# An attention's value products in one 65-column block of one bank, and a group's end in three instructions

## The chip, the core and the metric

The kernel runs on one core of one Trainium2 chip. The metric is device time in microseconds (us) of one execution. Five queues matter: TensorE (PE, with PEld for its weight loads), VectorE (DVE), ScalarE (ACT), GpSimd (POOL) and SyncE (SP), which issues most of the DMAs.

## The reference, cut to what matters

The program is one layer of an encoder on 2048 tokens of width 1024: an RMSNorm, one combined projection, latent attention with 12 heads (queries and keys of 64 + 32 rotary dimensions, values of 64), a small cross-attention to 256 memory rows, a silu gate, an output projection, the residual and a last RMSNorm. All in float32. What the change touches is this:

```
s = (einsum('bqhd,bkhd->bhqk', qn, k_nope) + einsum('bqhr,bkr->bhqk', qr, k_rope)) * scale
p = softmax(s, axis=-1)
attn = einsum('bhqk,bkhd->bqhd', p, v)
branch = concatenate([attn, mem_out], axis=-1) * silu(gate)
```

## The kernel before, in words

To keep float32's accuracy with float16 operands, every operand is split into a high part (the value rounded to float16) and a low part (what is left), and a product is made of three: high by high, high by low, low by high.

The work has three stages. First come the projections, the gate (its silu is written into float32 tiles A, 128 x 4 x 256 for each chunk of 512 tokens) and the memory heads. Then comes the latent attention, here read as the stretch from 461 to 1600 us. Last comes the output projection, to the end.

The attention runs over 48 groups: 6 pairs of heads, 4 chunks of 512 queries, 2 heads. A group has 16 units, one for each 128 keys. A unit (`scores`, then `pv` three units later) does this:

- Three 512-column matmuls make the scores of 128 keys by 512 queries in one bank (tag sc, three banks).
- ACT takes the exponential twice, once to float16 (the high part) and once to float32. Then DVE, or GpSimd in three units of eight, subtracts one from the other: the low part. In the trace this is a 128x512 TENSOR_TENSOR B<-B.
- The value product follows for each of the unit's four blocks of 128 queries. The high part is the stationary operand against 129 columns (64 of v's low part, 64 of v's high part, one column of a constant for the softmax's sum), and the low part against the last 65 of these. A tile of 129 columns per block results, two blocks to a bank, so a group holds both banks of the tag pv.

Beside the units, the groups ahead are prepared: 16 matmuls with 16 TENSOR_REDUCEs on DVE find the row maxima of the next group (tag m, three banks), and the next pair's keys, values and queries are projected (`prep_k`, `prep_v`, `prep_q_steps`), with ACT and DVE writing the high and low parts. GpSimd also splits the output projection's weights.

A group ends in `evac` once its last unit is added up. For each of the two banks ACT copies the low-part columns into a tile sm, DVE takes the reciprocal of the sums, DVE adds the high-part columns to sm, and then two SCALAR_TENSOR_TENSORs on DVE multiply each block by its reciprocal and by the gate tile, in place. The pair's banks come free when the two additions have read them.

The order on each engine is made at build time by a scheduler that lists the instructions against its own estimate of time; each engine then runs its list strictly in order. Matmuls go out in that order too (line 116 records them all, line 91 every instruction of DVE, ACT and GpSimd).

Of the kernel before, what the change touches and what calls it, by code (L numbers as in the profile page):

```python
# [9 lines left out]
F32 = mybir.dt.float32  # L10
# [3 lines left out]
ALU = mybir.AluOpType  # L14
# [3 lines left out]
P = 128  # L18
# [10 lines left out]
VD = 64  # L29
# [12 lines left out]
TPC = CH // P  # L42
# [3 lines left out]
XS = 16.0  # L46
XW = 1.0 / (XS * WS)
BS = 1.0 / 16.0
X_PART = {0: ((0, slice(0, 256)),), 1: ((0, slice(256, 1024)),), 2: ((1, slice(0, 512)),), 3: ((1, slice(512, 1024)),)}
X_JOIN = 2  # L50
DVE_TO = 4
# [19 lines left out]
def kernel(ctx: ExitStack, tc: tile.TileContext, a, out: bass.AP):  # L71
# [26 lines left out]
    vec, act, gps = Ordered(nc.vector), Ordered(nc.scalar), Ordered(nc.gpsimd)  # L98
# [6 lines left out]
    def T(tag, shape, dt):  # L105
        cnt[0] += 1
        return sb.tile(shape, dt, tag=tag, bufs=TAGS[tag], name=f"{tag}_{cnt[0]}")

    def PT(tag):
        cnt[0] += 1  # L110
        return ps.tile([P, 512], F32, tag=tag, bufs=TAGS[tag], name=f"ps_{tag}_{cnt[0]}")
# [3 lines left out]
    def mm(o, lhsT, rhs, start, stop):  # L115
        ins = nc.tensor.matmul(o, lhsT, rhs, start=start, stop=stop, skip_group_check=True)  # L116
        if strict[0]:
            tc.keep_in_program_order(ins)
        return ins
# [6 lines left out]
    def stt(o, i0, s, i1, op0, op1):  # L126
        vec.scalar_tensor_tensor(out=o, in0=i0, scalar=s, in1=i1, op0=op0, op1=op1)
# [79 lines left out]
        gps.tensor_tensor(pa, t2, c, op=ALU.mult)  # L207
        gps.tensor_tensor(t2, pa, pc, op=ALU.add)

# [1 line left out]
    gcol = sb.tile([P, 2 * NK], F32, name="gcol")  # L211
    nc.sync.dma_start(gcol, a["gcols"])
    junk = sb.tile([P, QL], BF16, name="junk")
# [53 lines left out]
        act.activation(ctab.rearrange("p t f -> p (t f)"), kf, AF.Sin)  # L267


# [1 line left out]
    ops = {}  # L271

    def hilo(dst, src, eng):
# [62 lines left out]
            ins = mm(o, hi[:, js_], wh, False, stop and j == 3)  # L336
        return ins

# [1 line left out]
    W1 = [T("B", [P, 2, NW1], F16) for _ in range(NK)]  # L340
    hTs = {}
    A = {}
# [127 lines left out]
            for o, i in late.pop(0)[1]:  # L470
                tc.keep_in_program_order(nc.sync.dma_start(o, i, transpose=True))

# [1 line left out]
    kmem = [None]  # L474
    vmem = [None]
    wms = {}
# [25 lines left out]
    def mem_acc(h, q):  # L502
        if h == 0 and q == 0:
            kmem[0] = T("V", [NOPE + 1, 2, 2, 2, NMEM], F16)
            gps.memset(kmem[0][NOPE:NOPE + 1, :, :, 0, :], -MROW)
            vmem[0] = T("cn", [P, 2, MHEADS, 2 * VD + 1], F16)
            gps.memset(vmem[0][:, :, :, 2 * VD:2 * VD + 1], 1.0 / BS)
        if q == 0:
# [90 lines left out]

    def pv(g, u):  # L600
        if u == 0:
            g.pv = [PT(g.pvtag), PT(g.pvtag)]
        phl = g.p.pop(u)
        last = u == g.nkeys // P - 1
        vl, vh = g.v(u)
        W = 2 * VD + 1
        for qt in range(TPC):
            o = g.pv[qt // 2]
            b = (qt % 2) * W
            mm(o[:, b:b + W], phl[:, 0, qt * P:(qt + 1) * P], vl, u == 0 and qt % 2 == 0, False)  # L610
            mm(o[:, b + VD:b + W], phl[:, 1, qt * P:(qt + 1) * P], vh, False, last)

    def norm_pair(o3):
        sm = T("sm", [P, 2, VD], F32)
        rc = T("st", [P, 2, 1], F32)
        acopy(sm, o3[:, :, 0:VD])
        vec.reciprocal(rc, o3[:, :, 2 * VD:2 * VD + 1])
        vec.tensor_tensor(sm, o3[:, :, VD:2 * VD], sm, op=ALU.add)
        return [(j, sm[:, j, :], rc[:, j, :]) for j in range(2)]

    def evac(g):
        W = 2 * VD + 1
        at = a_tile(g.c, g.col // 256)
        for i in range(2):
            o3 = g.pv[i][:, 0:2 * W].rearrange("p (q w) -> p q w", q=2)
            for j, sm, r in norm_pair(o3):
                gs = at[:, i * 2 + j, g.col % 256:g.col % 256 + VD]
                stt(gs, sm, r, gs, ALU.mult, ALU.mult)

    LAG = 3  # L630

# [26 lines left out]
    def mem_steps(t):  # L658
        st = {}
        W = 2 * VD + 1  # L660

# [76 lines left out]
    Vt = {}  # L738
# [37 lines left out]
    def alloc_v(p):  # L776
        Vt[p] = [T("V", [P, NT, 2 * VD + 1], F16) for _ in range(2)]
        for hd in range(2):
            gps.memset(Vt[p][hd][:, :, 2 * VD:2 * VD + 1], 1.0 / BS)

# [84 lines left out]
    def mla_group(p, hd, c):  # L865
        g = Group()
        g.kd = QKD
        g.c, g.col = c, (p * 2 + hd) * VD
        g.nkeys, g.dim, g.scale = SEQ, QKD, SC_MLA
        hi, lo = Kt[p][hd]  # L870
        g.khi = lambda o, n, e=0: hi[0:QKD + e, o:o + n]
        g.klo = lambda o, n: lo[0:QKD, o:o + n]
        qt = Qt[(p, hd, c)]
        g.qhi, g.qlo = qt[:, 0, :], qt[:, 1, :]
        g.v = lambda u: (Vt[p][hd][:, u, :], Vt[p][hd][:, u, VD:2 * VD + 1])
        g.p = {}
        g.last = (p, hd, c) == (NPAIR - 1, 1, NCH - 1)
        g.pvtag, g.sctag = "pv", "sc"
        g.alloc = mla_alloc
        return g  # L880
# [1 line left out]
    krT[:] = [T("B", [P, SEQ], F16), T("B", [P, SEQ], F16)]  # L882
    fq, hq = [], []

# [9 lines left out]
            if f is not None:  # L894
                f()

# [1 line left out]
    Wg = {}  # L898
    wgt, wgr, wgs = {}, {}, {}
    scr = {"b": dram.tile([P, 4, 3, 2, 512], F16, name="scr_b")}  # L900
# [126 lines left out]
    def reload_A(j, c):  # L1027
        nc.sync.dma_start(a_tile(c, j), spill[c, j - 1])

# [1 line left out]
    first = {}  # L1031

    def first_max():
# [166 lines left out]
            lambda: put("S4", comb(a12, a12, a11, ALU.subtract), gps),  # L1200
        ]

# [1 line left out]
    order = [(p, hd, c) for p in range(NPAIR) for c in range(NCH) for hd in range(2)]  # L1204
    cur = first["g"]
    wo_in = a["w_out_l0"]
# [67 lines left out]
    for n in range(12):  # L1274
        c, j = n % NCH, 1 + n // NCH
        wo_at.setdefault(A_AT[j] + c, []).append((0, lambda j=j, c=c: reload_A(j, c)))
    for n, name in enumerate(WO_BLK):
        g = (41 if n < 4 else 46) + n % 2
# [8 lines left out]
    for gi, (p, hd, c) in enumerate(order):  # L1287
        slots = [[] for _ in range(16)]
        j = gi % 8
# [4 lines left out]
        if hd == 0 or gi == len(order) - 7:  # L1294
            if hd:
                np_, nc_ = p, 2
            if np_ < NPAIR and nc_ < NCH:
                st = prep_q_steps(np_, nc_)
# [35 lines left out]
            cur = hold["g"]  # L1334
    stream.flush()

# [1 line left out]
    SC = IWS / BS  # L1338

    chain = [None]  # L1340
# [18 lines left out]
    for i in range(NT // 2):  # L1359
        strict[0] = i > 0  # L1360
        t0, t1 = 2 * i, 2 * i + 1
        last = i == NT // 2 - 1
# [36 lines left out]
    i, t0, t1 = NT // 2 - 1, NT - 2, NT - 1  # L1399
# [75 lines left out]
```

## Time and profile before

| | |
|---|---|
| median of 3 runs | 1766.88 us (1765.35 to 1768.74) |
| span of the profiled execution, first to last instruction | 1761.3 us |
| difference between the two | 5.6 us |
| busy over the span: PE, DVE, ACT, POOL | 95%, 84%, 73%, 53% |
| attention, 461 to 1600 us | 1139 us |
| granted clock of TensorE over the span / in the attention | 0.988 / 1.00 |

The span is of one profiled execution; the runs were timed apart from it, so the 5.6 us hold what lies before the first and after the last instruction and the spread of the runs. A matmul's row lasts until its last result is written, while the next one already streams, so PE's busy share is higher than the share of time in which it streams.

### The profile page before, as it was taken

Reading aid. Unit: us, or ns where it says so; the run is one execution under the profiler, and the core shown is the slowest. Engines: PE = TensorE matmul, PEld = TensorE weight load, DVE = VectorE, ACT = ScalarE, POOL = GpSimd, SP = SyncE. Lnnn points to the kernel's source line nnn. Section 1 sums busy time; section 2 is a strip of 40 time slices with the busy share of each in tenths; the row PEclk is TensorE's granted clock in tenths of the full one; section 3 lists DMA queues with packets and bytes.
Section 4 is the critical chain, followed back from the end, with each engine's and each line's share of the span. In section 5 each row is a group of like instructions: output and inputs, shape, how many; then the busy total and the mean of one; then the engine's idle time right before and its main releaser. Section 6 shows DMA issues by size and latency. Waiting matters only on the chain.

```text
span 1761.3 us, 38122 instructions
## 1 busy us (share of the span) xinstructions
PE 1677.2 (95%) x14292; PEld 935.8 (53%) x14292; DVE 1471.3 (84%) x2785; ACT 1279.6 (73%) x2642; POOL 926.3 (53%) x1211
## 2 busy tenths in 40 slices
PE   7999999989999999999999999999999999998997
PEld 3554544435455565566555655556556555554443
DVE  6777658777889889998999898988999889987775
ACT  6776657776788778878787777877888778884332
POOL 2766444443355556566665665555344455435553
PEclk9999989999999999999999999999999999999999
DMA  8753350221301012111211132113001134105774
GB/s 291 212 167 111 77 148 25 84 103 49 85 14 25 22 50 72 35 38 23 61 22 38 22 86 34 37 23 95 13 13 37 38 96 97 25 25 124 189 194 141
DMA packets 187034, 133.95 MB, mean 76 GB/s; under 512 B 140193, under 2 KB 162849, under 8 KB 186849
## 3 DMA queue, kind: packets, MB, share of 16 engines
q1 hardware_dynamic: 186560, 130.74, 28.2%
q8 instruction: 111, 1.82, 0.4%
q10 hardware_dynamic: 288, 0.79, 0.1%
q14 instruction: 75, 0.61, 0.1%
HBM read 69.89 MB, written 25.17 MB: 54 GB/s over the span
## 4 chain that ended last, share of the span: by engine, by line
PE 52%; DVE 23%; DMA 8%; ACT 8%; issue 5%; POOL 3%; SPq 0%; DVEq 0%; ACTq 0%; POOLq 0%
PE ps_sc L116 27%; PE ps_pv L116 13%; PE ps_m L116 12%; DVE B L91 11%; DVE st L91 9%; ACT B L91 6%; DMA W<-V 3%; DMA V<-in_x_dram 1%; POOL B L91 1%; DVE V L91 1%; DMA B<-V 1%; DMA W<-B 1%; DVE W L91 1%; DVE sm L91 1%; POOL V L91 1%
## 5 line engine op out<-in xcount | busy, mean ns | idle before, releaser
L116 PEld LDWEIGHTS <-B 128*128 128x128 f16 (+2 forms) x9720 | 638.0, 98 | 504.5 <-issue 47.2
L91 ACT ACTIVATE B<-ps_sc 128x512 f16<-128x512 f32 x1529 | 794.7, 619 | 142.8 <-PE ps_pv L116 84.8
L91 POOL TENSOR_TENSOR B<-B 128x512 f16<-128x512 f32 (+1 forms) x328 | 392.6, 1201 | 495.3 <-ACT B L91 420.1
L116 PE MATMUL ps_sc<-W,B 96*128 96x512 f16 (+1 forms) x2304 | 627.4, 379 | 6.3 <-ACT B L91 3.7
L91 DVE TENSOR_REDUCE st<-ps_m 128x1 f32<-128x512 f32 (+1 forms) x800 | 525.8, 680 | 72.6 <-PE ps_m L116 69.8
L91 DVE TENSOR_TENSOR B<-B 128x512 f16<-128x512 f32 (+1 forms) x494 | 400.7, 819 | 42.1 <-ACT B L91 34.7
L116 PE MATMUL ps_pv<-V,B 128*128 128x129 f16 (+1 forms) x6144 | 384.6, 207 | 16.9 <-DVE B L91 9.7
L116 PEld LDWEIGHTS <-W 128*128 128x128 f16 (+2 forms) x2164 | 205.3, 99 | 236.9 <-issue 38.4
L116 PE MATMUL ps_m<-B,W 96*128 96x512 f16 x768 | 273.6, 381 | 13.7 <-DVE st L91 11.2
L116 PE MATMUL ps_sc<-B,B 128*128 128x512 f16 (+1 forms) x912 | 212.6, 371 | 11.2 <-ACT B L356 6.5
L116 PE MATMUL ps_sc<-B,W 128*128 128x512 f16 x648 | 156.6, 391 | 13.5 <-DVE cn L91 8.3
L91 POOL TENSOR_TENSOR B<-B,B 128x256 f16<-128x256 f32 (+3 forms) x112 | 110.3, 985 | 88.0 <-DVE B L91 80.2
L91 ACT ACTIVATE W<-ps_m 1x512 f16<-1x512 f32 (+2 forms) x144 | 78.1, 542 | 59.9 <-PE ps_m L116 25.0
L91 ACT ACTIVATE B<-B 128x512 f32<-128x512 f32 (+4 forms) x132 | 79.8, 643 | 31.5 <-DVE B L91 15.3
L91 ACT ACTIVATE V<-B 128x256 f16<-128x256 f32 x112 | 40.8, 413 | 75.5 <-DMA W<-V 36.2
L116 PE MATMUL ps_m<-cT,W 128*128 128x512 f16 x360 | 87.7, 383 | 0.0
L116 PE MATMUL ps_sc<-cT,W 128*128 128x512 f16 (+1 forms) x312 | 71.7, 381 | 6.4 <-DVE B L91 6.4
L91 DVE SCALAR_TENSOR_TENSOR B<-sm,st,B 128x64 f32<-128x64 f32 x192 | 73.9, 432 | 0.0
L91 POOL TENSOR_TENSOR st<-st,mhalf 128x1 f32<-128x1 f32 x66 | 42.4, 643 | 58.5 <-DVE st L91 55.9
L116 PE MATMUL ps_m<-W,cT 128*128 128x64 f16 (+1 forms) x1440 | 71.4, 203 | 0.0
L116 PEld LDWEIGHTS <-cT 128*128 128x128 f16 x1440 | 64.5, 98 | 10.9
L91 POOL TENSOR_TENSOR V<-B,V 128x256 f16<-128x256 f32 x70 | 52.5, 768 | 31.9 <-ACT V L91 31.7
(123 smaller groups left out, 1554.0 us busy)
## 6 DMA issues: line engine op xcount, KB each, us to landing
B<-in_xT_dram SPq DMA_DIRECT2D x16, 512.0 KB, 7.3
V<-in_x_dram SPq DMA_DIRECT2D x16, 512.0 KB, 5.3
B<-in_x_dram SPq DMA_DIRECT2D x16, 512.0 KB, 4.7
V<-in_xT_dram SPq DMA_DIRECT2D x14, 512.0 KB, 4.1
wo_scr<-B SPq DMA_DIRECT2D x56, 128.0 KB, 2.0
out_dram<-B SPq DMA_DIRECT2D x14, 512.0 KB, 3.2
spill<-B SPq DMA_DIRECT2D x12, 512.0 KB, 2.8
B<-spill SPq DMA_DIRECT2D x12, 512.0 KB, 3.8
```

The lines of the kernel that those rows point to most:

```text
L91: ins = f(*args, **kw)
L116: ins = nc.tensor.matmul(o, lhsT, rhs, start=start, stop=stop, skip_group_check=True)
```

## The change

`pv` makes three products for each block of queries instead of two, all into the same 65 columns: high by v's high part and the sum's column (65 columns), high by v's low part (64 columns), low by v's high part (65 columns). The four blocks of a group lie side by side in one bank (4 x 65 = 260 columns), so a group holds one bank of the tag pv and not two. `evac` becomes one reciprocal over the four sums and one TENSOR_TENSOR on DVE that multiplies the four blocks by the gate tile, and one TENSOR_TENSOR on GpSimd that multiplies the result by the reciprocals. ACT has no part in a group's end any more. `norm_pair` stays for the memory heads. The columns streamed for a block are 129 + 65 = 194 before and 65 + 64 + 65 = 194 now; the matmuls and weight loads of the attention's value products go from 6144 to 9216 each.

```diff
+PVW = VD + 1
...
     def pv(g, u):
         if u == 0:
-            g.pv = [PT(g.pvtag), PT(g.pvtag)]
+            g.pv = PT(g.pvtag)
         phl = g.p.pop(u)
         last = u == g.nkeys // P - 1
         vl, vh = g.v(u)
-        W = 2 * VD + 1
         for qt in range(TPC):
-            o = g.pv[qt // 2]
-            b = (qt % 2) * W
-            mm(o[:, b:b + W], phl[:, 0, qt * P:(qt + 1) * P], vl, u == 0 and qt % 2 == 0, False)
-            mm(o[:, b + VD:b + W], phl[:, 1, qt * P:(qt + 1) * P], vh, False, last)
+            b = qt * PVW
+            o = g.pv[:, b:b + PVW]
+            hi, lo = phl[:, 0, qt * P:(qt + 1) * P], phl[:, 1, qt * P:(qt + 1) * P]
+            mm(o, hi, vh, u == 0 and qt == 0, False)
+            mm(g.pv[:, b:b + VD], hi, vl, False, False)
+            mm(o, lo, vh, False, last)
...
     def evac(g):
-        W = 2 * VD + 1
         at = a_tile(g.c, g.col // 256)
-        for i in range(2):
-            o3 = g.pv[i][:, 0:2 * W].rearrange("p (q w) -> p q w", q=2)
-            for j, sm, r in norm_pair(o3):
-                gs = at[:, i * 2 + j, g.col % 256:g.col % 256 + VD]
-                stt(gs, sm, r, gs, ALU.mult, ALU.mult)
+        gs = at[:, :, g.col % 256:g.col % 256 + VD]
+        o3 = g.pv[:, 0:TPC * PVW].rearrange("p (q w) -> p q w", q=TPC)
+        rc = T("st", [P, TPC, 1], F32)
+        vec.reciprocal(rc, o3[:, :, VD:PVW])
+        vec.tensor_tensor(gs, o3[:, :, 0:VD], gs, op=ALU.mult)
+        gps.tensor_tensor(gs, gs, rc.to_broadcast([P, TPC, VD]), op=ALU.mult)
...
-        g.v = lambda u: (Vt[p][hd][:, u, :], Vt[p][hd][:, u, VD:2 * VD + 1])
+        g.v = lambda u: (Vt[p][hd][:, u, 0:VD], Vt[p][hd][:, u, VD:2 * VD + 1])
```

The scheduler lists the instructions anew. On DVE, this is the end of the 22nd of the 48 groups before (ps_pv_13237 and ps_pv_13238 are the group's two banks, sm the tiles of the additions, st_13556 the row maxima of the next group, B_9006 the gate tile):

```order
L91 RECIPROCAL st_13597<-ps_pv_13237 128x2
L91 TENSOR_TENSOR sm_13596<-ps_pv_13237,sm_13596 128x128
L91 RECIPROCAL st_13604<-ps_pv_13238 128x2
L91 TENSOR_TENSOR sm_13603<-ps_pv_13238,sm_13603 128x128
L91 TENSOR_REDUCE st_13556<-ps_m_13700 128x1
L91 TENSOR_REDUCE st_13556<-ps_m_13703 128x1
L91 SCALAR_TENSOR_TENSOR B_9006<-sm_13596,st_13597,B_9006 128x64 x2
L91 TENSOR_REDUCE st_13556<-ps_m_13721 128x1
L91 SCALAR_TENSOR_TENSOR B_9006<-sm_13603,st_13604,B_9006 128x64 x2
L91 TENSOR_REDUCE st_13556<-ps_m_13740 128x1
```

And the end of the same group now, on DVE (ps_pv_14350 is its bank, st_14724 the row maxima of the next group, B_5246 to B_5249 the exponentials whose low parts are taken, B_9538 the gate tile):

```order
L92 TENSOR_REDUCE st_14724<-ps_m_14750 128x1
L92 RECIPROCAL st_14772<-ps_pv_14350 128x4
L92 TENSOR_TENSOR B_9538<-ps_pv_14350,B_9538 128x4x64
L92 TENSOR_TENSOR B_5247<-B_5247 128x512
L92 TENSOR_REDUCE st_14724<-ps_m_14827 128x1
L92 TENSOR_TENSOR B_5248<-B_5248 128x512
```

Eight instructions of the group's end have become two, and the two stand behind the third TENSOR_REDUCE of the next group, where the eight began behind the fifth.

On GpSimd the multiply by the reciprocals stands between the pieces of the weights' split, the next queries' rotation and the low parts, here at the same group's end (B_9538 is the gate tile, cn_14813 the queries' rotation, B_14043 and B_14463 the output projection's weights, B_5246 and B_5249 low parts of exponentials):

```order
L92 TENSOR_TENSOR B_14463<-B_14043,B_14463 128x256
L92 TENSOR_TENSOR B_5246<-B_5246 128x512
L92 TENSOR_TENSOR B_14043<-B_14043 128x256
L92 TENSOR_TENSOR B_9538<-B_9538,st_14772 128x4x64
L92 TENSOR_TENSOR cn_14813<-cn_14813,ctab 128x128
L92 TENSOR_TENSOR cn_14813<-cn_14813,stab 128x128 x2
L92 TENSOR_TENSOR B_5249<-B_5249 128x512
```

The row of B_9538 is new in this queue: it waits for DVE's multiply, and the rotation and the low part of B_5249 stand behind it.

## Rows read from the trace of the kernel before

**Rows 1.** The page: the chain that ended last, shares of the span.
```profile
PE 52%; DVE 23%; DMA 8%; ACT 8%; issue 5%; POOL 3%; SPq 0%; DVEq 0%; ACTq 0%; POOLq 0%
```
**Rows 2.** Busy time in the attention (stretch, its length; each engine's busy us; clock).
```profile
461.00:1600.00 1139.00, 1099.72 (x10987) 654.49 (x10986) 1025.37 (x1859) 911.12 (x1878) 623.01 (x651) 1.00 0.18 43
```
**Rows 3.** PE's instructions by form, 461 to 1600 us (count, busy us, mean ns, idle).
```profile
L116 PE MATMUL ps_m<-B,W 96*128 96x512 f16 x745 | 264.5, 380 | 13.7 <-DVE st L91 11.2 <-ACT W L91 0.7 <-DVE V L91 0.2
L116 PE MATMUL ps_m<-cT,W 128*128 128x512 f16 x327 | 78.4, 379 | 0.0
L116 PE MATMUL ps_m<-W,cT 128*128 128x128 f16 x480 | 32.7, 219 | 0.0
L116 PE MATMUL ps_m<-W,cT 128*128 128x64 f16 x792 | 30.1, 193 | 0.0
L116 PE MATMUL ps_m<-ident,st 128*1 128x128 f16 x188 | 18.0, 218 | 4.3 <-DVE st L91 2.6 <-DVE B L91 1.6
```
**Rows 4.** The same without splitting by form: the scores and the value products.
```profile
L116 PE MATMUL ps_sc<-W,B 96*128 96x512 f16 x2295 | 624.4, 379 | 4.7 <-ACT B L91 3.7
L116 PE MATMUL ps_pv<-V,B 128*128 128x129 f16 (+1 forms) x6144 | 384.6, 207 | 16.9 <-DVE B L91 9.7 <-ACT B L91 3.6 <-POOL B L91 2.1
```
**Rows 5.** PE's timeline at four places (start us, us, what, count).
```profile
649.81 0.95 PE L116 MATMUL ps_m<-W,cT 128*128 128x64 f16 x27
...
901.83 1.67 PE L116 MATMUL ps_m<-cT,W 128*128 128x512 f16 x7
...
906.10 0.51 PE L116 MATMUL ps_pv<-V,B 128*128 128x129 f16 x8
906.45 0.38 PE L116 MATMUL ps_sc<-W,B 96*128 96x512 f16 x1
```
**Rows 6.** Sum over 47 stretches: 9 us from each group's first reciprocal.
```profile
sum 423.00, PE 396.83 PEld 234.83 DVE 422.37 ACT 325.30 POOL 274.79; mean PE 8.44 PEld 5.00 DVE 8.99 ACT 6.92 POOL 5.85
```
**Rows 7.** Sum over 47 stretches: the 3 us after those.
```profile
sum 141.00, PE 140.13 PEld 85.07 DVE 135.77 ACT 111.58 POOL 73.21; mean PE 2.98 PEld 1.81 DVE 2.89 ACT 2.37 POOL 1.56
```
**Rows 8.** Waits of PE and its loads, 461 to 1600 us (total us, times, longest).
```profile
PE ps_m L116 <- DVE st L91: 13.8, 42, 1.2
...
PEld L116 <- DVE B L91: 37.8, 70, 1.8
...
PEld L116 <- ACT B L91: 8.5, 19, 0.7
```
**Rows 9.** The timeline behind the 22nd group's end.
```profile
989.26 0.96 DVE L91 SCALAR_TENSOR_TENSOR B<-sm,st,B 128x64 f32<-128x64 f32 x2
...
990.75 0.61 DVE L91 SCALAR_TENSOR_TENSOR B<-sm,st,B 128x64 f32<-128x64 f32 x2
990.88 0.38 PE L116 MATMUL ps_m<-B,W 96*128 96x512 f16 x1 [0.46 <-DVE st L91]
```
**Rows 10.** DVE's, ACT's and GpSimd's instructions by form, 461 to 1600 us.
```profile
L91 DVE RECIPROCAL st<-ps_pv 128x2 f32<-128x2 f32 x96 | 15.3, 159 | 2.9 <-ACT sm L91 2.0
...
L91 DVE TENSOR_TENSOR sm<-ps_pv,sm 128x128 f32<-128x128 f32 x96 | 25.7, 268 | 0.0
...
L91 DVE SCALAR_TENSOR_TENSOR B<-sm,st,B 128x64 f32<-128x64 f32 x189 | 71.4, 425 | 0.0
...
L91 ACT ACTIVATE sm<-ps_pv 128x128 f32<-128x128 f32 x96 | 23.6, 325 | 6.0 <-PE ps_pv L116 6.0
...
L91 DVE SCALAR_TENSOR_TENSOR V<-ps_m,V 128x256 f16<-128x256 f32 x40 | 16.6, 414 | 0.0
...
L91 DVE SCALAR_TENSOR_TENSOR W<-ps_m,W 64x512 f16<-64x512 f32 x46 | 31.5, 685 | 11.2 <-ACT W L91 10.5
...
L91 POOL TENSOR_TENSOR B<-B 128x256 f32<-128x256 f32 x34 | 33.2, 976 | 0.0
```
**Rows 11.** Low parts on DVE: all, and one on the timeline.
```profile
L91 DVE TENSOR_TENSOR B<-B 128x512 f16<-128x512 f32 x480 | 395.1, 830 | 42.1 <-ACT B L91 34.7 <-issue 3.2 <-PE ps_sc L116 1.5
...
1040.09 0.68 DVE L91 TENSOR_TENSOR B<-B 128x512 f16<-128x512 f32 x1
```

## The prediction

> **What bounds the kernel now.** I read the chain of waits first. PE holds 52% of it and DVE 23% [rows 1], so the question is how often PE has to wait for DVE. The change touches the attention alone, 1139 us [rows 2]; the other stages keep their code. There PE shows 1099.7 us busy, which looks like 39 us of idleness. But a matmul's row is longer than its place in the stream. Seven 512-column matmuls take 1.67 us of rows, so one follows the other after (1.67 - 0.38) / 6 = 0.215 us, while its own row lasts 0.38 [rows 5]. So I count the stream itself [rows 3, 4]:
>
> - 2295 + 745 + 327 matmuls of 512 columns at 0.215 us: 723.9 us.
> - 768 units of value products. One unit's eight start at 906.10 and the next matmul at 906.45 [rows 5], 0.35 us: 268.8 us.
> - 792 of 64 columns. 27 of them take 0.95 us of rows, (0.95 - 0.19) / 26 = 0.029 us each [rows 3, 5]: 23.1 us.
> - 480 + 188 of 128 columns, an estimate of 0.056 us each (64 more columns at the 512-column rate, 0.215 / 512 us, on top of 0.029): 37.4 us.
>
> The sum is 1053 us, so PE stands still for some 86 of the 1139, 2.2 times what its busy time shows. Most of the waits that are named are for DVE: 37.8 and 13.8 us, against 8.5 for ACT [rows 8].
>
> Where does it stand still? I cut out 9 us from each group's end, 47 times. DVE is busy there for 422.4 of 423 us and PE shows 26.2 us of idleness. In the 3 us that follow it shows 0.9 of 141, or 2.6 in 423 [rows 6, 7]. So 24 of the 39 us shown stand behind a group's end, with DVE full. By the factor of 2.2 that is an estimate of 50 us really lost there. One such place: four SCALAR_TENSOR_TENSORs stand between the row maxima, and PE waits 0.46 us for a maximum at 990.88, while DVE multiplies blocks by gates [rows 9].
>
> **The change, part by part.** The parts are PE's products, the end of a group on DVE, on ACT and on GpSimd, the banks, and the order.
>
> *PE.* Each block of queries gets three products in place of two, 9216 in place of 6144, each with its weight load. The columns stay at 776 a unit. The nearest rows are the 64-column products, which also have a load each and also add three by three into the same columns: 0.0292 us. At the rate per column (0.00042 us), 65 columns make 0.0296. A unit then takes 8 x 0.0296 + 4 x 0.0292 = 0.354 us against 0.35: 768 x 0.004 = 3 us more. The lower end is 0 (equal columns). The upper end is an added product that costs its whole 0.029 us with nothing given back by the narrower ones: 3072 x 0.029 = 89 us. I take 3, since the 27 products in a row are the same shape in everything but one column.
>
> *DVE.* A group loses two reciprocals (0.159), two additions (0.268) and four multiplies (71.4 / 189 = 0.378 us of busy time each): 0.32 + 0.54 + 1.51 = 2.37 us [rows 10]. It gains a reciprocal over four sums, about 0.16, and a multiply of 256 columns of a bank by the gate. Nothing in the trace is exactly that. From below stands the 128-column addition (0.268), from above a 512-column SCALAR_TENSOR_TENSOR (0.685), nearest a 256-column one out of a bank (0.414) [rows 10]. I take 0.41. Net: 1.8 us a group (1.5 to 1.9), 86 us in 48 groups.
>
> What is that worth? DVE is full exactly where it goes, so PE's waits there can shrink until PE or ACT is the last. The 50 us lost, by DVE's share of the three named waits (51.6 of 60.1, 86%), are 43; 1.8 x 47 = 85 us of relief is enough for all of them. But it is not spread evenly, and other low parts of 0.685 us (keys, values, queries) stay in the same stretch. I take seven tenths, 30 us. The ends are 0 (another DVE instruction is late just the same) and 60 (the rest of the attention gains too).
>
> *ACT.* Two copies of 0.325 go, 31 us in all [rows 10]. ACT is busy for 325 of 423 us behind a group's end [rows 6], so this is worth little: I count 2 us, between 0 and the 8.5 us that the loads wait for ACT.
>
> *GpSimd.* One multiply of 128x256 a group is added. Its nearest row is 0.976 us [rows 10], 47 us in all, and GpSimd is busy for 623 of 1139 us. Nobody but the output projection reads the gate tile, so the multiply is hidden as such. It waits for DVE's multiply, and what stands behind it in the queue is a low part that PE needs three units later and the next queries' rotation. It also slows DVE: a low part takes 0.68 us on the timeline when it is quick and 0.830 in the mean [rows 11]. If all of that comes from GpSimd's work, 480 x 0.15 = 72 us over 623 us of it, then 47 us more cost DVE 5 us. I count 2 us of time, between 0 and what the third rival gives.
>
> The Trainium skill says more here (SBUF — State Buffer, Who interferes with whom): a DVE instruction with two operands in SBUF and a GpSimd instruction that reads SBUF take the same port, and the second waits out the first. The mean of 0.830 against 0.68 agrees in direction; by the rule each multiply could hold a low part for its full 0.976 us, and the sum above would then keep 39 of DVE's 86 us, some 14 us of gain in place of 30.
>
> *Banks and order.* A group now holds one of the two banks, so the next group's first product no longer waits for `evac`. No row in the groups shows a large wait for that, so I count 0. The scheduler places the two DVE instructions two maxima earlier; I count that as 0 too, with 5 us either way.
>
> The sum is 1761.3 - 30 - 2 + 3 + 2 = 1734.3 us of span. The runs' median lies 5.6 us above the span, so 1740 us.
>
> **The rivals.**
>
> *DVE was the bound of the whole attention.* For: DVE is busy for 1025 of 1139 us, and 136 of 141 even after the crowded 9 us. Against: PE shows almost no idleness there. If PE's 86 us shrink to 30, the gain is 56 with 3 us of cost: 1714 us.
>
> *More products cost PE more than DVE gives back (slower).* PE is the engine at its limit, and weight loads or the issue of 24 instructions a unit in place of 16 may not keep up over a whole attention, as they do over 27 products. The place is the end of every `pv`. It decides from (30 + 2 - 2) / 3072, about 10 ns for each added product. At 20 ns it is 61 us against 30 of gain: 1767 + 31 = 1798 us. Against it stands the pitch of 0.029 us with a load for each product.
>
> The Trainium skill has a rule that would make this rival certain (TensorE: Matmul & The Clock Gate, Back-to-back issue gap): where the sequencer decodes matmuls by itself it spends about 62 ns on each, whatever the columns. By it a unit's twelve would take 0.74 us, against a trace in which eight take 0.35 and 27 follow each other at 0.029; the trace contradicts it here, and I give it 1 of 100 inside this rival's chance.
>
> *GpSimd gives DVE's time back.* The multiply falls where GpSimd is busy for 275 of 423 us [rows 6]. If each holds up a low part of 0.976 us on DVE, or delays one of GpSimd's own that PE then waits for, 47 us come back on the engine that is full. Of its relief 39 of 86 us are left, so at least 16 of the 30 us of gain go, at most all: between 1756 and 1770 us, say 1763.
>
> **How the numbers follow.** My forecast of 1740 us (1726 to 1756) has a chance of 58%, DVE as the whole bound (1714) 15%, GpSimd giving it back (1763) 14%, PE's products (1798) 10%, and 3% is left for an order that turns out otherwise. About 0.2%, 3.5 us, is what a measurement of this kernel can tell from no change. Faster by more are the first two, half of the third and 1%: 81%. Within it is most of the other half: 6%. Slower: 10% with 1% of the third and 2% of the rest, 13%. The range goes from 1712, just below the second case, to 1769, above the third.
>
> **What would show it.** Right: value products of 64 and 65 columns at a pitch of 0.029 to 0.030 us, and units of twelve in about 0.35; DVE's busy time in the attention down by some 85 us; PE's waits for DVE's maxima and low parts about halved; GpSimd up by some 45 us. Wrong on PE, if twelve take 0.45 us or more. Wrong on DVE, if it loses its 85 us and PE's waits stay, which would mean that something other than a full DVE made the maxima late. Wrong on GpSimd, if the mean of DVE's low parts rises well above 0.83, or PE waits for low parts of GpSimd.

## The result and the profile after

The changed kernel takes 1737.37 us (median of 4 runs, 1736.28 to 1738.93) against 1767.81 us for the kernel before in the same session: ratio 0.9828 [0.9808, 0.9848], 30.4 us less. The forecast was 1740. The profiled execution took 1738.93 us, 2.0 more than its span of 1736.9. The span is 24.4 us shorter than before's: with the same 2 us around it, before's profiled execution took some 1763 us, one of its quicker ones, so spans show less than medians.

The busy time by stage in the profiled execution after (start and end, length; busy us of PE, PEld, DVE, ACT, POOL; granted clock, DMA share, GB/s). The middle row answers [rows 2]:

```profile
0.00:461.00 461.00, 431.52 (x2636) 215.17 (x2637) 332.74 (x700) 312.02 (x628) 221.32 (x466) 0.96 0.40 122
461.00:1575.00 1114.00, 1100.48 (x14067) 672.47 (x14066) 945.97 (x1577) 908.63 (x1787) 652.23 (x701) 1.00 0.19 45
1575.00:1736.00 161.00, 142.82 (x665) 64.75 (x663) 109.82 (x223) 54.35 (x133) 81.60 (x94) 0.99 0.74 173
```

All of the gain is in the attention: 1139 us have become 1114, and the first and last stage are as long as they were. DVE lost 79 us there and GpSimd got 29 more. PE is busy for as long as before, in a stretch that is 25 us shorter. The same 47 stretches of 9 us from each group's first reciprocal as in [rows 6], after:

```profile
sum 423.00, PE 420.64 PEld 258.61 DVE 395.39 ACT 379.98 POOL 330.30; mean PE 8.95 PEld 5.50 DVE 8.41 ACT 8.08 POOL 7.03
```

This is the plainest picture of what happened. DVE was full there (422 of 423) and is not now, and PE's idleness went from 26.2 us to 2.4. PE's instructions in the attention, the shapes of a group together (count, busy us, mean ns, idle us before them and who ended it), against [rows 3, 4]:

```profile
L117 PE MATMUL ps_sc<-W,B 96*128 96x512 f16 (+1 forms) x2297 | 641.6, 379 | 4.1 <-ACT B L92 3.7
L117 PE MATMUL ps_pv<-V,B 128*128 128x65 f16 (+1 forms) x9216 | 442.6, 193 | 7.8 <-DVE B L92 4.1 <-POOL B L92 3.5
L117 PE MATMUL ps_m<-B,W 96*128 96x512 f16 x746 | 265.0, 381 | 0.7 <-DVE st L92 0.6
L117 PE MATMUL ps_m<-cT,W 128*128 128x512 f16 x327 | 78.1, 379 | 0.0
L117 PE MATMUL ps_sc<-cT,W 128*128 128x512 f16 x21 | 5.1, 379 | 0.0
```

Waits of PE, its loads and DVE (total us, times, longest), against [rows 8]:

```profile
PEld L117 <- DVE B L92: 18.4, 35, 1.8
...
PEld L117 <- ACT B L92: 0.6, 1, 0.6
...
PE ps_m L117 <- DVE st L92: 1.3, 4, 0.6
...
DVE st L92 <- PE ps_m L117: 88.5, 122, 1.9
```

PE's wait for row maxima was 13.8 us and is 1.3; the loads' wait for low parts has halved (37.8 to 18.4). DVE now waits 88.5 us for PE to deliver the scores whose maxima it takes: the two have changed places.

One unit of value products on PE's timeline (start, us, what, count), as in [rows 5]; then a group's end on DVE, a low part on DVE and the new multiply on GpSimd, as in [rows 10, 11]:

```profile
902.30 0.53 PE L117 MATMUL ps_pv<-V,B 128*128 128x65 f16 x12
902.66 0.60 PE L117 MATMUL ps_sc<-W,B 97*128 97x512 f16 x2
```

```profile
L92 DVE RECIPROCAL st<-ps_pv 128x4 f32<-128x4 f32 x48 | 8.4, 176 | 2.6 <-PE ps_pv L117 2.6
L92 DVE TENSOR_TENSOR B<-ps_pv,B 128x256 f32<-128x256 f32 x48 | 18.9, 394 | 0.0
...
L92 DVE TENSOR_TENSOR B<-B 128x512 f16<-128x512 f32 x480 | 387.9, 810 | 54.4 <-ACT B L92 36.2 <-POOL B L92 5.7 <-issue 4.8
...
L92 POOL TENSOR_TENSOR B<-B,st 128x256 f32<-128x256 f32 x47 | 38.2, 812 | 6.5 <-PE ps_m L117 4.7 <-DVE B L92 1.7
```

Twelve products take 0.36 us, where eight took 0.35. Over the whole attention the difference is larger. From one start to the next, averaged over the value products that follow each other at once, a block took 58.1 + 30.0 = 88.1 ns before (129 columns, then 65) and takes 31.8 + 29.1 + 31.8 = 92.7 ns now (65, 64, 65). With 3072 blocks that is 14 us more on PE's stream, or 12 where a unit's first product, which is slower in both kernels, is left out. So the stream, counted as in the prediction, is 3391 matmuls of 512 columns at 0.215 us (729.1), 3072 x 0.0927 (284.8) and the same 23.1 + 37.4: 1074 us. PE stands still for 40 of 1114 us. Before, counted in the same way (with 16 matmuls of 512 columns that my count had left out, 3.4 us, and 88.1 ns a block), it was 80 of 1139.

### The profile page after: what moved, and what is told of

The parts are those of the page before. It is cut to its first block, busy times and chain, and to the rows that moved or that the text cites. A ratio compares the mean times of both kernels' runs of the same rounds, so it can differ in the third digit from the quotient of the medians.

```text
span 1736.9 us, 43935 instructions
## 1 busy us (share of the span) xinstructions
PE 1674.8 (96%) x17364; PEld 952.4 (55%) x17364; DVE 1388.5 (80%) x2497; ACT 1275.0 (73%) x2546; POOL 955.1 (55%) x1259
## 5 line engine op out<-in xcount | busy, mean ns | idle before, releaser
L117 PEld LDWEIGHTS <-B 128*128 128x128 f16 (+2 forms) x12792 | 673.5, 98 | 487.7 <-issue 26.2
L92 ACT ACTIVATE B<-ps_sc 128x512 f16<-128x512 f32 (+1 forms) x1529 | 799.8, 609 | 137.4 <-PE ps_sc L117 96.5
L117 PE MATMUL ps_sc<-W,B 96*128 96x512 f16 (+1 forms) x2304 | 643.8, 379 | 5.7 <-ACT B L92 3.7
L92 POOL TENSOR_TENSOR B<-B 128x512 f16<-128x512 f32 (+1 forms) x328 | 386.0, 1181 | 442.3 <-ACT B L92 389.0
L117 PE MATMUL ps_pv<-V,B 128*128 128x65 f16 (+1 forms) x9216 | 442.6, 193 | 7.8 <-DVE B L92 4.1
L92 DVE TENSOR_TENSOR B<-B 128x512 f16<-128x512 f32 (+1 forms) x494 | 393.5, 800 | 54.4 <-ACT B L92 36.2
L117 PEld LDWEIGHTS <-V 128*128 128x128 f16 (+2 forms) x664 | 41.7, 96 | 34.7 <-issue 6.2
```

The lines of the kernel that those rows point to most:

```text
L92: ins = f(*args, **kw)
```

## The experiments

The expectations name the theories by letters. A is the forecast's: a lighter DVE behind a group's end lets PE go on, and what PE pays for the added products is small. B: the gain comes from the products, the banks or the order. C: an added product costs PE its whole time. D: GpSimd's new work takes back the time that DVE gains. E: DVE is still the bound after the change. F, where banks are compared: the freed bank carries much of the gain; F in the kernel without the multiplies: they are worth little on DVE. Each ratio is to the kernel before, run in the same session; differences in us are ratios times 1767, and a difference between two of these kernels is good to some 5 us.

**The new products alone, with a group's end as heavy as before.** Two banks, and copies, reciprocals, a DVE operation over 128 columns (where the addition stood, the maximum of a value and its own copy, which leaves it as it is) and four multiplies as before:

```diff
+            g.pv = [PT(g.pvtag), PT(g.pvtag)]
...
+            acopy(sm, o3[:, :, 0:VD])
+            vec.reciprocal(rc, o3[:, :, VD:PVW])
+            vec.tensor_tensor(sm, o3[:, :, 0:VD], sm, op=ALU.max)
+            for j in range(2):
+                stt(gs, sm[:, j, :], rc[:, j, :], gs, ALU.mult, ALU.mult)
```

> The three products of a block in 65 columns, but two banks and the group's end of before (ACT copies, DVE takes the larger of the block and its copy in place of the sum, so the same instructions as before on ACT and DVE). Theory A (the gain is DVE's relief behind a group's end, the products themselves cost PE a little): slower than before by 3 to 9 us, 1771 to 1777 us, DVE busy in the attention as before (1025 us). Rival B (the gain comes from the products, the narrower block in PSUM, or the new order they lead to): faster than before by 10 us or more. Rival C (an added product costs PE its whole 0.029 us): slower by up to 89 us, 1850 us.

Measured: 1777.06 us, 1.0061 [1.0037, 1.0085], 10.8 us slower than before. A's term of 3 us is too small; the pitch alone would make 12 to 14. Some 3 of the 10.8 lie in the last six groups, where the accident told of below stands (132.7 us against 129.8).

**The same in one bank.** `g.pv` is one bank; all else as in the kernel just told of.

> The three products with the group's end of before (ACT copies, the larger of block and copy in place of the sum, four multiplies on DVE), but in one bank instead of the two of the first experiment. Theory A: the bank is worth nothing, so as there, 1772 to 1782 us. Rival F: the next group starts early, so faster than there by 15 us or more, 1762 us or less.

Measured: 1771.26 us, 1.0020 [1.0004, 1.0035], 7 us less than with two banks and nearer to A than to F. The prediction had counted the bank at nothing. The two kernels are not alike in DVE's work, though the instructions are the same. The four multiplies, first with two banks and then with one:

```profile
L92 DVE SCALAR_TENSOR_TENSOR B<-sm,st,B 128x64 f32<-128x64 f32 x189 | 70.7, 416 | 0.0
```

```profile
L92 DVE SCALAR_TENSOR_TENSOR B<-sm,st,B 128x64 f32<-128x64 f32 x189 | 97.2, 552 | 0.0
```

DVE is busy for 1015 us of the attention in the first and for 1035 in the second, so the 7 us are what is left when DVE has some 20 us more to do.

**The changed kernel in two banks.** Products as after; the reciprocal and the gate's multiply once for each bank:

```diff
-            g.pv = PT(g.pvtag)
+            g.pv = [PT(g.pvtag), PT(g.pvtag)]
...
+        for i in range(2):
+            vec.reciprocal(rc[:, s], o3[:, :, VD:PVW])
+            vec.tensor_tensor(gs[:, s], o3[:, :, 0:VD], gs[:, s], op=ALU.mult)
```

> The changed kernel, but a group's four blocks lie in two banks as before (two blocks of 65 columns each), with a reciprocal and a multiply by the gate for each bank: one reciprocal and one half-size multiply more on DVE, some 0.3 us a group, 14 us. Theory A (the relief of DVE is the gain; the banks are worth nothing): 0 to 7 us slower than the changed kernel, 1737 to 1744 us. Rival F (the free second bank lets the next group's products start while the last group is still being read, and that is a good part of the gain): 15 us slower or more, 1752 us and up.

Measured: 1749.42 us, 0.9904 [0.9883, 0.9924], 13 us slower than after, between the two expectations. DVE's two extra instructions a group hardly explain it: they take 13.6 us (15.2 + 25.7 in place of 8.4 + 18.9), but its busy time in the attention is 948 us against 946, since its low parts are quicker. Held against after group by group, the profiled execution falls behind in a few places only. It loses 5.2 us in the stretch between two groups' reciprocals from 884.54 to 914.92 us (30.4 us against 25.2), some 3 around the one from 741.31 to 768.78, and 2.1 in the first. From 914.92 on the two run level, 11.5 us apart there and 12.0 at the last group. In the longest of these places ACT waits for the queries' transfer, PE stops for ACT, and then PE's granted clock is low (a row of ACT, one of PE, and a stretch with the columns of the first table):

```profile
903.93 0.59 ACT L92 ACTIVATE W<-ps_m 64x512 f16<-64x512 f32 x1 [4.36 <-DMA W<-B]
...
905.53 0.81 PE L117 MATMUL ps_sc<-W,B 96*128 96x512 f16 x3 [2.18 <-ACT B L92]
...
906.00:913.00 7.00, 6.95 (x56) 3.78 (x55) 3.79 (x8) 3.74 (x8) 1.84 (x2) 0.52 0.00 1
```

Around 759 us ACT waits for such transfers for 3.41 and 1.51 us. So with the light end no cost of the second bank shows that comes back in every group; most of the 13 us is how the order fell in two or three places, as in the accident told of below. Against the heavy end in two banks, the light end gains 28 us; in one bank (after against the kernel above) it gains 34, with the longer multiplies of that kernel in it.

**The end alone.** The old products and banks; the four multiplies go to GpSimd, two for each bank:

```diff
+            gps.tensor_tensor(gs, sm, gs, op=ALU.mult)
+            gps.tensor_tensor(gs, gs, rc.to_broadcast([P, 2, VD]), op=ALU.mult)
```

> The products and banks of before; at a group's end the four multiplies leave DVE and become four multiplies of 128x128 on GpSimd (two by the gate, two by the reciprocals). DVE loses 1.5 us a group, 72 us, GpSimd gains some 2.2 us a group, 106 us. Theory A: 72 of the 79 us that DVE lost in the changed kernel, without the products' cost, so faster than before by 22 to 30 us, 1738 to 1746 us. Rival B (the gain is the products' or the banks'): no change, 1764 to 1771 us. Rival D (GpSimd's work on the shared gate takes DVE's time back): faster by less than 12 us, 1756 us or more.

Measured: 1755.97 us, 0.9941 [0.9921, 0.9962], 10 us faster: a miss for A, and what D had said. What was saved on DVE stands on GpSimd (first rows), and PE stands longer before its scores, for ACT's exponentials (last row; 4.7 us before, [rows 4]). In the next kernel, which has no such work on GpSimd, that is 8.6 us, so this wait does not tell the two apart.

```profile
L91 POOL TENSOR_TENSOR B<-B,st 128x128 f32<-128x128 f32 x94 | 45.9, 500 | 0.9
...
L91 POOL TENSOR_TENSOR B<-sm,B 128x128 f32<-128x128 f32 x94 | 43.7, 475 | 32.4 <-DVE sm L91 29.6 <-DVE st L91 2.8
...
L116 PE MATMUL ps_sc<-W,B 96*128 96x512 f16 x1532 | 460.5, 381 | 10.7 <-ACT B L91 10.1
```

**The four multiplies gone.** The kernel leaves out the multiplies by the gate and the reciprocals. This tells D, a cost on GpSimd, from F, multiplies that are worth little on DVE:

```diff
-                stt(gs, sm, r, gs, ALU.mult, ALU.mult)
...
+            vec.tensor_tensor(gs, o3[:, :, VD:2 * VD], sm, op=ALU.add)
```

> The kernel before without the four multiplies of a group's end: DVE's sum goes straight into the gate tile, and the multiplies by gate and reciprocals are left out of the computation. DVE loses 72 us as in the second experiment, GpSimd gains nothing. Theory A with GpSimd in its way there: faster than before by 20 to 30 us, 1736 to 1747 us. Rival F (DVE's multiplies are worth only the 10 us seen there, the rest is the banks or ACT's copies): 1753 to 1760 us.

Measured: 1744.67 us, 0.9881 [0.9851, 0.9910], 21 us faster. F falls, and D holds for these kernels: 72 us of DVE's work, taken away with nothing put elsewhere, give back 21 us, 0.29 us for each; moved to GpSimd they give back 10. The 11 us between are then the price of 90 us of new work on GpSimd, with the order that was listed for it. The attention of the two, in one row each:

```profile
461.00:1593.00 1132.00, 1103.67 (x11000) 659.78 (x10998) 956.01 (x1669) 907.74 (x1878) 697.10 (x843) 0.99 0.18 44
```

```profile
461.00:1582.00 1121.00, 1098.90 (x11000) 658.90 (x10999) 952.38 (x1673) 908.08 (x1882) 620.99 (x655) 1.00 0.19 44
```

DVE is relieved alike (956 and 952 us); GpSimd is not (697 and 621). The price does not come evenly. One stretch between two groups' reciprocals, from 695.90 to 726.44 us with the multiplies on GpSimd, takes 30.5 us there and 24.1 without them. GpSimd is full at its start, and ACT and PE behind it go as in the place above:

```profile
697.00:709.00 12.00, 12.00 (x121) 7.13 (x118) 11.05 (x18) 10.47 (x23) 11.92 (x16) 1.00 0.21 57
...
714.35 0.59 ACT L91 ACTIVATE W<-ps_m 64x512 f16<-64x512 f32 x1 [4.34 <-DMA W<-B]
...
717.00:721.00 4.00, 3.81 (x24) 1.76 (x24) 2.58 (x6) 3.18 (x7) 1.78 (x2) 0.59 0.00 0
```

**The reciprocals' multiply on DVE in place of GpSimd**, in the changed kernel:

```diff
-        gps.tensor_tensor(gs, gs, rc.to_broadcast([P, TPC, VD]), op=ALU.mult)
+        vec.tensor_tensor(gs, gs, rc.to_broadcast([P, TPC, VD]), op=ALU.mult)
```

> The changed kernel with the multiply by the reciprocals on DVE instead of GpSimd: DVE gains some 0.42 us a group, 20 us, GpSimd loses 38 us. Theory A (a microsecond of DVE behind a group's end is worth about 0.4 us of time): 5 to 12 us slower than the changed kernel, 1742 to 1750 us, ratio to before 0.986 to 0.990. Rival D (GpSimd's multiply holds DVE's low parts up by as much as it saves): the same as the changed kernel or faster, 1737 us or less, ratio 0.983 or less.

Measured: 1737.79 us, 0.9828 [0.9804, 0.9852], the same as after, though DVE got 36 us of work: a miss for A, and what D had said. The new instruction, and the attention:

```profile
L92 DVE TENSOR_TENSOR B<-B,st 128x256 f32<-128x256 f32 x47 | 36.3, 772 | 0.8
```

```profile
461.00:1580.00 1119.00, 1107.39 (x14102) 676.32 (x14101) 968.60 (x1632) 908.13 (x1788) 612.56 (x659) 1.00 0.19 46
```

DVE's busy time went from 946 to 969 us and GpSimd's from 652 to 613, and the two cancel. That GpSimd takes the third instruction is not what makes the change pay. That DVE's microseconds alone cost nothing now is not shown: by the prices of the kernel before, an estimate, 23 us on DVE would cost 7 and 40 us off GpSimd would give back 6 (11 us for 76 of busy time), which cancel as well. No run puts work on DVE alone.

**A fourth product, low by v's low part, 64 columns**, on PE alone:

```diff
+            mm(g.pv[:, b:b + VD], lo, vl, False, False)
```

> The changed kernel with a fourth product a block, low part by v's low part, into the same 64 columns: 3072 matmuls more, 90 us of streaming at 0.0292 us each. Theory A (PE is the bound now, with about 50 us of standing still left): most of it shows, 60 to 90 us more than the changed kernel, 1797 to 1827 us. Rival E (DVE is still the bound after the change): PE has room for it, less than 30 us more, under 1767 us. A pitch above 0.035 us in the trace would speak for a limit of weight loads or issue, with over 110 us more.

Measured: 1819.04 us, 1.0297 [1.0272, 1.0322], 83 us slower than after. 3072 products of 0.0292 us [rows 3] are 90 us; nine tenths of them show. So PE's stream bounds the attention now, as A had said and against E, and this also shows what the 10% rival would have cost if each added product had taken its whole time.

```profile
902.43 0.66 PE L117 MATMUL ps_pv<-V,B 128*128 128x65 f16 x16
902.93 0.38 PE L117 MATMUL ps_m<-B,W 96*128 96x512 f16 x1
```

Sixteen take 0.50 us, twelve 0.36.

**Why 31.8 ns for 65 columns, where before they took 30.0?** Now every second block begins at an odd column; so one kernel puts the four blocks at columns 0, 128, 256 and 384:

```diff
-            b = qt * PVW
+            b = qt * P
```

> The changed kernel with the four blocks of 65 columns at columns 0, 128, 256 and 384 of the bank instead of 0, 65, 130 and 195. In the changed kernel 65 columns follow at 31.8 ns in the mean (64 at 29.1), where 29.6 were expected. If the blocks' odd starts in the bank make the difference: 29.6 ns, 6144 x 2.2 ns = 13 us of PE's stream less, 1724 to 1731 us. If it has another cause (the weights change from one block to the next): the same as the changed kernel, 1734 to 1740 us, 31.8 ns.

Measured: 1743.4 us, 0.9872 [0.9852, 0.9893], and the pitch stayed at 31.9 ns: refuted. It is even some 8 us slower than after; the one execution with a profile was the quickest of the four (1736.35 us) and runs level with after's, so no trace shows why. The next one changes the order of the three products (64 columns first; it also holds the edit told of at the end of this section, so it is to be compared with that one):

```diff
-            mm(o, hi, vh, u == 0 and qt == 0, False)
-            mm(g.pv[:, b:b + VD], hi, vl, False, False)
+            mm(g.pv[:, b:b + VD], hi, vl, u == 0 and qt == 0, False)
+            mm(o, hi, vh, False, False)
```

> The changed kernel (blocks side by side) with the branch in order as in the run before, and the first two products of a block exchanged: v's low part (64 columns) first, then v's high part and the low part's product (65 columns each). In the runs so far the second 65 columns behind 64 take 33.4 to 33.6 ns and the first 65 behind 65 take 29.7. If the slow place goes with the change from 64 to 65 columns or from one half of v to the other, it moves or goes: a mean of 29.5 to 30.5 ns, 4 to 8 us less, 1722 to 1726 us. If it goes with the block's last product, it stays: 31.8 ns and 1728 to 1732 us.

Measured: 1727.45 us, 0.9780 [0.9766, 0.9793], equal to the last kernel of this section. But the slow place moved. After, the gaps from the start of each of the three products to the next start are 29.7, 29.0 and 33.4 ns (without a unit's first product); here the 65 columns that start behind the 64 take 33.3 ns. With the fourth product (65, 64, 64, 65) it is the last that takes 33.3. In all three orders it is the 65 columns that follow 64. A block costs the same: 29.8 + 2 x 31.5 = 92.8 ns. So the place goes with the order of shapes; why is not settled.

**An accident of the order.** One group of the changed kernel takes 31.6 us between its reciprocals (from 1439.54 to 1471.18 us) where its neighbours take 20 to 25. The timeline of that place, PE and one row of ACT (in brackets what each waited for):

```profile
1457.10 0.53 PE L117 MATMUL ps_pv<-V,B 128*128 128x65 f16 x12
...
1458.45 0.59 ACT L92 ACTIVATE W<-ps_m 64x512 f16<-64x512 f32 x1 [4.62 <-DMA W<-B]
...
1460.06 0.81 PE L117 MATMUL ps_sc<-W,B 96*128 96x512 f16 x3 [2.42 <-ACT B L92]
...
1461.61 0.54 PE L117 MATMUL ps_pv<-V,B 128*128 128x65 f16 x12 [0.68 <-DVE B L92]
...
1462.79 0.58 PE L117 MATMUL ps_m<-ident,st 128*1 128x128 f16 x4 [0.64 <-DVE st L92]
...
1464.99 0.87 PE L117 MATMUL ps_pv<-V,B 128*128 128x65 f16 x12
1465.66 1.04 PE L117 MATMUL ps_sc<-W,B 96*128 96x512 f16 x2
```

And three stretches around it, with the columns of the first table:

```profile
1440.00:1452.00 12.00, 11.96 (x152) 7.03 (x149) 10.38 (x17) 9.85 (x22) 11.94 (x15) 1.00 0.01 2
1455.00:1460.00 5.00, 2.63 (x44) 1.70 (x41) 0.93 (x2) 1.55 (x3) 0.07 (x1) 1.00 1.09 151
1463.00:1466.00 3.00, 3.00 (x21) 1.48 (x19) 1.62 (x3) 2.50 (x6) 2.41 (x3) 0.50 0.95 280
```

GpSimd is full for twelve microseconds (11.94), with the queries' rotation and the split of the first tokens' gated branch, an operand of the output projection, which the scheduler listed here, four groups ahead of its place in the program. The rotated queries are turned by a DMA that is therefore late. ACT waits 4.62 us for it, and the exponentials stand behind it in its queue. PE stops for 2.42 us and then for 0.68 and 0.64, and from 1463 us on its granted clock is 0.50, the level of 1.2 GHz: twelve products take 0.67 us in place of 0.36. Starting the queries of the last groups later in their group (unit 15, not 11) leaves them further from their use:

```diff
-                for u, s in zip((2,11), st):
+                for u, s in zip((2, 15 if gi >= 41 else 11), st):
```

> The changed kernel with the last two chunks' queries (the part of 64 dimensions) projected at unit 15 of a group instead of 11, so that ACT's writing of them no longer waits 4.6 us for the rotary part's transpose, behind which PE stood still for 2.6 us and then ran at half its clock. If that wait is a cost by itself: 4 to 9 us faster than the changed kernel, 1728 to 1733 us. If the time is lost to the transposes' lateness in another place: the same as the changed kernel, 1735 to 1740 us.

Measured: 1735.18 us, 0.9819 [0.9793, 0.9844]; not to be told from after. The group takes 27.8 us there, and ACT waits 3.70 us for another such transfer, the values'. The other way keeps the branch's split in program order, from two groups before its old place in the program on, which puts it behind the crowded group:

```diff
-BR_AT = (46, 2, 2)
+BR_AT = (44, 2, 4)
...
+            pin[0] = True
+            f()
+            pin[0] = False
```

first with the blocks at 128 columns:

> The same, and the first tokens' gated branch is split at a fixed place in the order (from group 44 on) instead of where the scheduler lists it, so that GpSimd and the transposes are free for the last queries at group 42. If the crowding there costs 4 to 8 us: that much faster than the run with the blocks at 128 columns alone. If the work is only moved to where it crowds something else: no difference beyond 3 us.

Measured: 1729.96 us, 0.9791 [0.9774, 0.9808], 14 us less than with the blocks at 128 columns alone, more than was expected. And alone:

> The changed kernel with the branch in order alone (blocks side by side, products in the changed kernel's order): the reference for the exchange of products. If the 128-column places are worth nothing, the same as the run with both: 1728 to 1733 us.

Measured: 1727.44 us, 0.9782 [0.9767, 0.9798], some 8 us better than after: it beats both kernels. Its attention takes 1101 us, and the group of the accident 23.8:

```profile
461.00:1562.00 1101.00, 1093.08 (x14051) 669.35 (x14050) 941.75 (x1570) 904.27 (x1779) 648.57 (x695) 1.00 0.18 45
```

The accident helps to read the others. The six groups from that one to the last take 129.8 us before, 134.3 after, 126.8 in this last kernel; 132.7 and 134.4 for the heavy end in two banks and in one, 133.9 for after in two banks, 136.5 with the multiplies on GpSimd, 134.2 without them and 137.8 with the reciprocals' multiply on DVE (one profiled execution each). So 4 to 7 us of what the two kernels of the old products failed to gain lie there. None of the bank's 13 us with the light end does; those lie in the places shown above.

## Why the prediction was right, and where its terms were off

The direction, the place and the size were right: a full DVE behind a group's end made PE wait, and it was relieved. Of the signs that the prediction named, the waits for maxima and low parts fell by half and more, DVE's busy time fell by 79 us (85 expected), and a unit of twelve takes 0.36 us (0.35). Two came out otherwise: 65 columns follow at 31.8 ns, not at 29 to 30, and GpSimd got 29 us more, not 45. The third rival's sign did not appear: the low parts' mean went from 0.830 to 0.810 us. But that the sum met the measured time so closely is luck: it came out through errors that cancel.

Two readings of the rows were loose, without changing the sum. In [rows 9] PE's 0.46 us before 990.88 pass while DVE takes the maximum itself, in a row that those do not show; the multiplies stand before and behind it:

```profile
990.15 0.68 DVE L91 TENSOR_REDUCE st<-ps_m 128x1 f32<-128x512 f32 x1
```

And DVE's 86% of the named waits leave out the loads' idle time without a releaser, which is nearly as large as the largest of them; it fell too, from the first of these rows to the second:

```profile
PEld L116 <- issue: 36.0, 93, 1.1
```

```profile
PEld L117 <- issue: 13.6, 40, 2.5
```

- **The products (+3 us).** Mis-sized: 10.8 us by the kernel that has them alone (some 3 of them in the accident's groups), 12 to 14 by the pitch. I took 65 columns in a mixed row to follow as 64 alike do; they take 31.8 ns, not 29.6. The rival that this makes the kernel slower had its point of decision at 10 ns for each added product, of which a block has one; measured are 4 to 5 ns a block. The Trainium skill (TensorE: Matmul & The Clock Gate, Back-to-back issue gap) gives for the gap of a lone matmul its columns over 2.4 GHz plus 2.5 ns, by estimate 29.2 ns for 64 and 29.6 for 65. The trace has 29.1 for 64, 30.0 for 65 behind 129, and 31.8 here, so the estimate comes close for 64 columns and falls short for 65 in this mixture.
- **The end of a group (-30 on DVE, -2 on ACT, +2 on GpSimd).** Right in sum: 28 us in two banks and 34 in one. The weight that I gave DVE's relief, 30 of 86 us or 0.35 each, was measured as 0.29 where it was taken away alone. That PE would be the next bound is shown by the fourth product, which also speaks against the rival that made DVE the bound of the whole attention (1714 us). Whether DVE's time is worth anything now is open, as said at the reciprocals' multiply.
- **GpSimd's multiply.** Priced at 0.976 us, measured 0.812. As a term it was small, as said: moving it to DVE changes nothing. The rival that GpSimd gives the time back did not come true with 38 us of work, but with 90 us of it (the multiplies alone) 11 of 21 us went that way, 6 of them in the one stretch shown. The prediction's reason for a price was right: before, a low part on DVE takes 0.68 us where no GpSimd instruction overlaps it in time (173 of 480) and 0.91 in the mean where one does.
- **The bank (0).** Too small as a term, right as a cost that recurs: one bank in place of two was worth 7 us with the heavy end and 13 with the light one, but with the light end most of it lies in two or three places of the order, and behind the 19th group the two kernels run level. The reason for the 0 was that no row showed a large wait for `evac`. What an absent wait doesn't show is the order: the scheduler had already listed the value products late where a bank was due late. In the listed order the first products of 154 of 768 units stand behind the scores of four or more later units before (three is the aim), nearly all of them among a group's first seven; 151 with the new products in two banks, 19 in one, 12 after, 25 after in two banks. With the heavy end the late order goes when the bank does, and 7 us with it, while DVE's multiplies get longer; with the light end it is gone already in two banks. No run held the order fixed, so what the bank does by itself with the heavy end is open.
- **The order (0, 5 either way).** It cost about 8 us in one group, shown by the two kernels that keep the branch's split in order: wrong by more than its 5 us. Nothing in the order of the places that I had looked at pointed there, 450 us behind them.

Put together: 10.8 (products) - 7 (one bank) - 34 (light end) is -30, what was measured; by way of two banks it is 10.8 - 28 - 13. These are steps from the kernel before to the one after, so their sum has to come out and proves nothing by itself. The forecast had 3 + 0 - 30 and reached -27.

## What to carry to other kernels

When an engine is full just where another one waits, count its relief at a fraction (here 0.3 us of time for each us taken away), and once the other engine's stream leaves little gap, count what is added to that stream nearly in full (here nine tenths). A buffer that shows no wait may still shape the order that a scheduler lists, so count what stands late in the list. Hold two kernels against each other group by group before you give a difference to its supposed cause: a single stretch that has become longer than its neighbours may hold most of it. And take the pitch of an instruction from a mixture like the one to come, not from a row of equals.

## What the hardware showed that I had not expected

- Three products of 65, 64 and 65 columns, each with a load, take 92.7 ns whichever goes first, and one of the gaps is 33.3 to 33.4 ns where the others are 29 to 30; it is always that of the 65 columns which start behind 64. Where the columns start in the bank makes no difference to it.
- Some DVE instructions on operands in SBUF are long only beside GpSimd. The multiply of 128x256 by the reciprocals, 772 ns in the mean, is one of two kinds (shortest, median and longest in ns):

```profile
L92 DVE TENSOR_TENSOR B<-B,st x47: 410/946/1251, 493.1 to 1553.3; 128x256 f32<-128x256 f32 x47
```

  Of the 48 in the whole trace, the 11 that no GpSimd instruction overlaps in time take 410 to 417 ns each; the other 37 take 869 in the mean. So neither the repeated operand nor the place makes it slow by itself. The row maxima, which read a bank alone, take 680 in the mean with a GpSimd instruction beside them or not.
- The scaling of the row maxima (TENSOR_SCALAR, 128x4), which the change doesn't touch, became quicker:

```profile
L91 DVE TENSOR_SCALAR st<-st 128x4 f16<-128x4 f32 x47 | 21.6, 459 | 0.5
```

```profile
L92 DVE TENSOR_SCALAR st<-st 128x4 f16<-128x4 f32 x47 | 9.2, 196 | 0.3
```

  That is 12 us less of DVE's time, before above and after below. The reason is the same: alone it takes some 160 ns in both kernels, and a GpSimd instruction overlaps 19 of the 47 before (900 ns in the mean) and 7 after.
- After stops of 2.42, 0.68 and 0.64 us on PE the granted clock was at its lower level, 1.2 GHz, for the 3 us from 1463 on, though PE was busy for all of these. In the changed kernel in two banks it was at 0.52 from 906 to 913 us behind a single stop of 2.18 us.
